# Attention transfers in program order, output weights gated and split in the stage before, and the attention output split where it is merged: one change to a two-layer trunk kernel on one core

## The chip, the cores and the metric

The kernel runs on one core of one Trainium2 chip. The metric is the device time of one launch in microseconds (us). Before the change the median of three runs is 2780.15 us, with 2775.05 as the lowest and 2784.62 as the highest.

The engines are named as the profile names them: PE is TensorE's matrix unit, PEld its weight loads, DVE is VectorE, ACT is ScalarE, POOL is GpSimd, SP is SyncE, which does little here but issue transfers. SPq and POOLq are the queues of transfers that SP and GpSimd issue.

## The reference: what must be computed

A sequence of 1024 tokens of width 1024 goes through two layers. Each layer has a token mixer and a dense MLP (1024 to 4096, squared ReLU, back to 1024). Every one of the four sub-layers is wrapped in the same way: `h = x * (1 + scale) + shift`, `x = LayerNorm(alpha * x + gate * f(h))`, where shift, scale and gate come from a conditioning vector. Layer 0 mixes with a gated MLP (mixer a), layer 1 with attention (mixer b). The change touches mixer b alone:

```
qkv = (h @ w_qkv)                      # 3 patterns x (q, k, v) x 16 heads x 64
for each pattern g (window, dilation) in (128,1), (512,4), (2048,16):
    s = q k^T / 8 + ALiBi bias          # 128 queries x 256 keys a block
    m = max(s);  p = exp(s - m);  l = sum(p)
    o_g = (p / l) v;   lse_g = m + log(l)
o = sum_g softmax_g(lse) * o_g          # the merge of the three patterns
y = o @ w_out;  x = LayerNorm(alpha * x + gate * y)
```

All is fp32. A matrix product is made of three passes in a rounded format: each operand is split into a high part (a cast on ACT) and a low part (a subtraction on DVE), and high*high, high*low and low*high are added up. The helper `split` (L100 to L104) issues the two instructions, L102 on ACT and L103 on DVE.

## The kernel before, in words

**The stages, in order of time.** Mixer a and its output projection; the MLP of layer 0 (`mlp(1)`); `values` (L1133), which makes v for all three patterns, and q and k of pattern 0, by a seven-product scheme; `attention` (L1279); the output projection of the attention; the MLP of layer 1 (`mlp(3)`). PE works in the order in which the program text issues. The order on the other engines is set by a scheduler, which takes an instruction when its operands are expected, unless the program pins it with `tc.keep_in_program_order`. The queue of an engine is then worked strictly in that order: an instruction that waits holds all that is behind it, transfers included.

**`values`.** The loop over `V_STEPS` (L1247) takes five blocks of seven products (numbered 1, 2, 5, 6, 7, 4, 3), each product four m-steps, each m-step twelve matmuls. After an m-step `evict` (L1217) either copies the sum to `vpart` (ACT, products 1, 5 and 6) or finishes it: an add on DVE, a split into a tile `vs` (two buffers, pool `parted`), and a store from GpSimd's queue to `v_dram` or `qk_dram` (L1233, L1240). The right-hand weights come through `raw_tile` buffers (two of tag "raw", three of tag "res").

**`attention`.** Eight pairs of heads times three patterns, in the order g = 0, 2, 1, make 24 groups of 8 slots, 4 slots for a head. Each slot has two half positions, and `at(slot, pos)` hangs a step on one. For head e of a group starting at slot `base`:
- `scores(m)` at base + 4e + m: four matmuls into `sc` (L1454, L1455), a bias add with row minimum on DVE into p (L1461), an exponential on ACT (L1463). For m = 0 it also issues the bias row on GpSimd (L1443), just ahead of its first use.
- `transposes(m)` (L1486) and its split into `pThi`, `pTlo` at base + 4e + w + 2, second half, where w is 0 to 3; `weighted(m)` (the `pv` matmuls, L1510, then the sum into `oT`, L1519 and L1520) two slots or more later. For g = 0 the last two m share one half slot (w = 3 for both).
- `statistics` (L1530) at base + 9 stores the row maxima and sums; for g = 0 they go through a transpose into `pstat` first (L1534 to L1536).

Between these steps a generator `project` is stepped: it loads the q and k weights of the coming groups (`unit`, L347), splits them and multiplies (`psq`, `psk`, L1366). A table `due` says how far it must be by a slot; its last entry is `last_group - 2`, with `last_group` = 184, the first slot of the last group.

**The merge** (`merge`, L1546) of a head pair begins when its three patterns are through. Steps on the slots of the next groups: `read` of the statistics, `late maths` for the three weights (L1567 to L1577), a store to `w_dram`, `spread`, which reads them back as rows `bc` across 64 partitions, and ten steps of scaling and adding on DVE (L1601, L1605). The sum of pairs 0 to 6 is stored to `o_dram` in fp32.

**The affine rows.** During the first groups GpSimd multiplies and adds the LayerNorm rows of the residual (L1637 load, two L1642 operations of 128x1024, L1643 store, eight rows one after the other).

**The output projection.** `OutRows` (L400) works on the eight 128-row units of `b_w_out`. `begin` does units 0 to 3 for tokens of the first half; its matmuls (`psd_wo`, L389) are stepped one at each half slot of the last group. `go_on` (L427) does the second half with units 0 and 1, then 2 and 3, then units 4 to 7 on both. A unit is loaded raw, multiplied by the row `gate_2` (GpSimd, L1688 for units 0 to 3, L356 for 4 to 7), and split (`wo_hi`, `wo_lo`). `prepare` (L1652) and `staged_rows` (L1701) load o from `o_dram` and split it into `oTs`. Units 6 and 7 have buffers `late_w`.

Of the kernel before, what the change touches and what calls it, by code (L numbers as in the profile page):

```python
# [10 lines left out]
F32 = mybir.dt.float32  # L11
# [6 lines left out]
P = 128  # L18
# [17 lines left out]
def trunk(ctx: ExitStack, tc: tile.TileContext, x, c, ada_w, ada_b, ln_g, ln_b, a_w_in, a_b_in,  # L36
# [168 lines left out]


# [140 lines left out]
    def unit(src, name, gate=None, pinned=False, lo_engine=V, to=None, raw=None):  # L347
        if raw is None:
            raw = wts.tile([P, D], F32, name=f"{name}_raw", tag="raw", bufs=2)[:]
        if src.shape[0] == P:  # L350
            nc.sync.dma_start(raw, src)
        else:
            nc.sync.dma_start(raw.rearrange("p (k n) -> p k n", n=P), src.rearrange("(k p) n -> p k n", p=P))
# [46 lines left out]
    class OutRows:  # L400
# [3 lines left out]
        def __init__(self, stat, weight, gate, res, prepare, name, raws={}):  # L404
            self.units = {}

            def load(ch):
                self.units[ch] = [unit(weight[k * P : (k + 1) * P, :], f"{name}_{k}", gate, ch > 1, raw=raws.get(f"w{k}"))
                                  for k in (2 * ch, 2 * ch + 1)]
# [10 lines left out]
            self.load, self.part, self.prepare, self.res, self.raws = load, part, prepare, res, raws  # L420
# [6 lines left out]
        def go_on(self):  # L427
# [6 lines left out]

            part((0,), 1)
            self.prepare(2)
# [4 lines left out]
            self.prepare(3)  # L441
            self.load(3)
            add(4, 5)
            part((2, 3), 0)
# [3 lines left out]
    def mixer_a():  # L448
        nonlocal ada_p, vec
        with ExitStack() as ph:  # L450
# [175 lines left out]
            with ExitStack() as a2:  # L626
# [9 lines left out]
                out = OutRows(uzT, a_w_out[0], gate, res, prepare, "wout")  # L636
# [435 lines left out]
    v_dram = [dram.tile([S, N_PAIRS, 4 * HEAD], F32, name=f"v_{g}") for g in range(3)]  # L1072
    qk_dram = [dram.tile([2 * N_PAIRS, 2, HEAD, S], F32, name=f"{n}_0") for n in "qk"]
# [59 lines left out]
    def values(before, right, ahead):  # L1133
# [3 lines left out]
        with ExitStack() as ph:  # L1137
# [104 lines left out]

            for n, (of, p) in enumerate(V_STEPS):
                while name[p] not in built:
                    next(stream)
                for m in range(4):
# [32 lines left out]
    def attention(form):  # L1279
        nonlocal vec  # L1280
        o_dram = dram.tile([N_PAIRS - 1, P, S], F32, name="o_dram")
# [3 lines left out]
        with ExitStack() as ph:  # L1285
# [55 lines left out]
            def project():  # L1341
# [3 lines left out]
                def load(n, X):  # L1345
                    hp, g = order[n]
                    c0 = g * 3 * D + X * D + hp * P
                    return unit(b_w_qkv[0, :, c0 : c0 + P], f"w{'qk'[X]}_{hp}_{g}", raw=raw_u[:])
# [34 lines left out]
            def load_qk(n):  # L1383
                hp = order[n][0]
                q, k = ([wts.tile([P, S], F32R, name=f"{nm}{e}_{hp}_0", tag=tag) for e in range(2)] for nm, tag in (("q", "whi"), ("k", "wlo")))
                for e in range(2):
                    rows = [d[2 * hp + e].rearrange("s c t -> (s c) t") for d in qk_dram]
                    nc.sync.dma_start(k[e][:].bitcast(F32), rows[1])
                    for i in range(2):
                        nc.sync.dma_start(q[e][64 * i : 64 * i + 64, :].bitcast(F32), rows[0][0:64])  # L1390
                    nc.sync.dma_start(zlo[e][0:64, :].bitcast(F32), rows[0][64:P])
# [14 lines left out]
            def attend(n, oT_of):  # L1406
# [6 lines left out]
                def load_v(e):  # L1413
# [4 lines left out]
                    if g == 0:  # L1418
                        nc.sync.dma_start(dst, src.rearrange("(t p) c -> p t c", p=P))
                    elif g == 1:  # L1420
                        for i in range(2):
                            nc.sync.dma_start(dst[:, i::2, :], src.rearrange("(i p r) c -> i p r c", i=2, r=4)[i])
                    else:
                        for b in range(2):
                            nc.sync.dma_start(dst[64 * b : 64 * b + 64], src.rearrange("(i b a) c -> b i a c", b=2, a=8)[b])
# [7 lines left out]
                for e in range(2):  # L1433
# [4 lines left out]
                    def scores(m, e=e, h=h, rows=rows, probs=probs, st=st):  # L1438
                        if m == 0:
                            if e == 0:  # L1440
                                my["stat"] = qp.tile([P, 2, 2, NT], F32, name=f"stat_{hp}_{g}", tag="stat", bufs=3)
                            st["bias"] = qp.tile([P, width], F32, name=f"bias_{h}_{g}", tag="bias")
                            G.tensor_scalar(st["bias"][:], far if g == 2 else near,  # L1443
                                            -8.0 * DILATION[g] * 2.0 ** (-8.0 * (h + 1) / N_HEADS), 1.0, ALU.mult, ALU.mult)
# [76 lines left out]

                    for m in range(4):
# [285 lines left out]
```

## Time and profile before

| | |
|---|---|
| median of three runs | 2780.15 us (2775.05 to 2784.62) |
| the profiled execution | 2781.12 us |
| its span in the trace | 2779.4 us |
| PE busy, in us and as a share of the span | 2668.7, 96% |
| DVE busy | 2036.6, 73% |
| ACT busy | 1419.5, 51% |
| POOL busy | 238.3, 9% |
| transfers | 483.78 MB, 174 GB/s mean |

The profile has one page for the whole span (busy time by engine, forty slices, the costliest groups of instructions by line) and views that can be asked of the trace: the waits of an engine by what ended them, busy times in chosen stretches with the granted clock of PE (1.00 is full speed), the chain of work that ended last, and a timeline of one engine. In the trace of before, `values` runs from about 995 to 1382 us, the slots of the attention from there to about 2060, the output projection to about 2145. A group of 8 slots takes some 26 us, so a slot takes about 3.25 us, and `last_group` begins at about 2026 us.

### The profile page before, as it was taken

The page shows a single profiled execution, that of the slowest core. Times are in us where ns is not written, and L with a number is a line of the kernel's source. Part 1 is how long each engine was busy: PE and PEld are TensorE (multiplying, and loading weights), DVE is VectorE, ACT ScalarE, POOL GpSimd, SP SyncE. Part 2 cuts the span into 40 slices and gives each one's busy share as a digit, 9 for nine tenths or more (in the row PEclk, how much of TensorE's full clock was granted, in tenths as well). Part 3 has the DMA queues.
Part 4 walks back from the last instruction along what each step waited for, and adds up shares of the span by engine and source line. Part 5 has one row for each costly group of instructions (what it writes and reads, how often), then busy time and mean ns, then how long its engine had stood idle before and what let it go on. Part 6 is the DMA issues. An engine that isn't in the chain of part 4 may idle for free.

```text
span 2779.4 us, 36657 instructions
## 1 busy us (share of the span) xinstructions
PE 2668.7 (96%) x12858; PEld 2222.1 (80%) x12858; DVE 2036.6 (73%) x3638; ACT 1419.5 (51%) x2655; POOL 238.3 (9%) x261
## 2 busy tenths in 40 slices
PE   6999999999999999999997999999988999999998
PEld 5787788887888878888886888878877788878887
DVE  6777698777877787655555777777768975668887
ACT  3354475555443464434364666666664755554332
POOL 1001000000000012211144011101120000000000
PEclk9999999999999999999998999999999999999999
DMA  7544347667846546655465455555444564486562
GB/s 258 162 124 124 114 138 235 214 219 263 315 139 195 169 144 205 207 201 201 154 202 147 124 135 123 138 131 131 120 127 159 166 209 153 159 284 212 172 200 90
DMA packets 344574, 483.78 MB, mean 174 GB/s; under 512 B 51981, under 2 KB 185525, under 8 KB 344389
## 3 DMA queue, kind: packets, MB, share of 16 engines
q1 hardware_dynamic: 329764, 430.05, 49.6%
q0 software_dynamic: 14624, 51.39, 5.4%
q8 instruction: 101, 1.65, 0.3%
q14 instruction: 85, 0.69, 0.1%
HBM read 355.44 MB, written 125.91 MB: 173 GB/s over the span
## 4 chain that ended last, share of the span: by engine, by line
PE 68%; DVE 14%; DMA 7%; ACT 5%; issue 3%; POOL 2%; SPq 0%; DVEq 0%; ACTq 0%; POOLq 0%
PE psd L955 21%; PE psv L1265 10%; PE psua L796 8%; PE psuc L796 4%; PE psu L368 3%; PE psq L1366 3%; PE psk L1366 3%; PE psd_wout L389 2%; PE psd_wo L389 2%; DMA adaw<-in_ada_w_dram 2%; PE psv L470 2%; PE psub L796 2%; PE pv L1510 2%; ACT p L1463 1%; POOL aff L1642 1%
## 5 line engine op out<-in xcount | busy, mean ns | idle before, releaser
L796 PE MATMUL psua<-right,left 128*128 128x512 f32 x1536 | 364.8, 391 | 0.3
L955 PE MATMUL psd<-rhi,lhi 128*128 128x512 f32 x896 | 349.2, 390 | 3.0 <-ACT part L827 3.0
L955 PE MATMUL psd<-rlo,lhi 128*128 128x512 f32 x896 | 348.9, 389 | 0.2
L955 PE MATMUL psd<-rhi,llo 128*128 128x512 f32 x896 | 348.6, 389 | 0.0
L796 PEld LDWEIGHTS psua<-right,left 128*128 128x128 f32 x1536 | 288.0, 188 | 62.5 <-DVE right L103 1.6
L1463 ACT ACTIVATE p<-p,stat 128x128 f32<-128x128 f32 (+1 forms) x384 | 170.7, 445 | 182.6 <-DVE stat L1461 168.5
L955 PEld LDWEIGHTS psd<-rhi,lhi 128*128 128x128 f32 x896 | 168.2, 188 | 38.8 <-ACT part L827 3.9
L955 PEld LDWEIGHTS psd<-rlo,lhi 128*128 128x128 f32 x896 | 168.2, 188 | 35.6 <-DVE rlo L103 1.1
L955 PEld LDWEIGHTS psd<-rhi,llo 128*128 128x128 f32 x896 | 168.2, 188 | 35.0
L796 PE MATMUL psuc<-right,left 128*128 128x512 f32 x768 | 187.5, 391 | 0.0
L128 DVE SCALAR_TENSOR_TENSOR adaacc<-adaw,silu_c,adaacc 128x512 f32<-128x512 f32 x168 | 132.2, 797 | 59.1 <-DMA adaw<-in_ada_w_dram 58.7
L796 PEld LDWEIGHTS psuc<-right,left 128*128 128x128 f32 x768 | 143.6, 188 | 30.0 <-DVE right L103 0.4
L103 DVE TENSOR_TENSOR left<-ws,left 128x512 fp32r<-128x512 f32 x128 | 87.8, 687 | 72.9 <-ACT left L102 71.3
L1461 DVE CUSTOM_DVE_ANT_0 p<-sc,bias 128x128 f32<-128x128 f32 (+1 forms) x384 | 119.0, 343 | 29.4 <-POOL bias L1443 20.2
L103 DVE TENSOR_TENSOR llo<-lraw,lhi 128x1024 fp32r<-128x1024 f32 x112 | 136.4, 1217 | 0.8 <-ACT lhi L102 0.8
L102 ACT CAST left<-ws 128x512 fp32r<-128x512 f32 x128 | 79.1, 620 | 96.5 <-DVE ws L717 86.6
L1366 PE MATMUL psk<-form_L,wk_hi 128*128 128x512 f32 x384 | 126.7, 411 | 0.0
L1366 PE MATMUL psq<-form_L,wq_hi 128*128 128x512 f32 x384 | 126.0, 410 | 0.0
L103 DVE TENSOR_TENSOR pTlo<-pT,pThi 128x384 fp32r<-128x384 f32 (+1 forms) x160 | 98.4, 620 | 32.1 <-ACT pThi L102 30.7
L102 ACT CAST rhi<-rraw 128x1024 fp32r<-128x1024 f32 x48 | 50.6, 1053 | 139.6 <-issue 114.1
L1520 DVE TENSOR_TENSOR oT<-oT,pv 64x512 f32<-64x512 f32 x96 | 65.8, 685 | 74.9 <-ACT oT L1519 74.1
L1265 PE MATMUL psv<-vrhi,form_S 128*128 128x512 f32 x384 | 119.2, 389 | 0.0
(311 smaller groups left out, 6478.1 us busy)
## 6 DMA issues: line engine op xcount, KB each, us to landing
lraw<-forms SPq DMA_DIRECT2D x112, 512.0 KB
adaw<-in_ada_w_dram SPq DMA_DIRECT2D x192, 256.0 KB
up<-in_mlp_w_up_dram SPq DMA_DIRECT2D x64, 512.0 KB
forms<-s SPq DMA_DIRECT2D x128, 256.0 KB
rraw<-in_mlp_w_down_dram SPq DMA_DIRECT2D x64, 512.0 KB
forms<-part SPq DMA_DIRECT2D x96, 256.0 KB
v<-vs POOLq DMA_DIRECT2D x48, 512.0 KB, 3.3
vraw<-in_b_w_qkv_dram SPq DMA_DIRECT2D x42, 512.0 KB
```

The costliest lines, as they stand in the source:

```text
L102: first = A.copy(hi, src) if hi_engine is A else hi_engine.tensor_copy(hi, src)
L103: return first, lo_engine.tensor_tensor(lo, src, hi, op=ALU.subtract)
L128: ins = V.scalar_tensor_tensor(acc[:], raw[:], silu_c[:, k : k + 1], acc[:], ALU.mult, ALU.add)
L368: T.matmul(dst, s[a], m[b], start=(n == 0), stop=(n == last))
L389: T.matmul(p[:], stat[a][:, k, o : o + P], u[b][:, w], start=n == 0, stop=n == count - 1)
L796: T.matmul(acc, w[:, a, k, :], right[p][:, b, k, :], start=p in (1, 2, 5) and k + a + b == 0, stop=k == 3 and a == 1, skip_group_check=True)
L955: ins = T.matmul(sums[kind, m][:], l[a][:, k, m * P : (m + 1) * P], r[b][:, k, :], start=p in (1, 5, 2, 3) and kp + k + a + b == 0, stop=k ...
L1265: T.matmul(acc, stat, mov, start=p in (1, 2, 5) and kp + k + a + b == 0, stop=kp == 1 and k == 1 and a == 1, skip_group_check=True)
L1366: T.matmul(p[:], wu[a][:, k * P : (k + 1) * P], h_op(k, half, b), start=k + c_ == 0, stop=k == KD - 1 and c_ == 2)
L1461: V.tensor_tensor_reduce(out=pr[:, 0:w], in0=scb[:, sl], in1=st["bias"][:, width - w :], scale=-0.125, scalar=3e38, op0=ALU.add, op1=ALU.m ...
L1463: A.activation(pr[:, 0:w], pr[:, 0:w], AF.Exp, bias=nm, scale=-1.0, accum_out=l)
L1520: V.tensor_tensor(dst, dst, pvs[b][main, :], op=ALU.add)
```

## The change

It has these parts.

1. **`in_turn`.** All transfers of the attention that SP issues (weights of q and k, q and k of pattern 0, v, the statistics, the merge's stores and reads, o) are pinned to program order on SP's queue.
2. **Output weights beside v.** In blocks 1 to 4 of `values`, a table `side` hangs steps on m-steps: load half of the gate row, load two 128-row units by 512 columns of `b_w_out` (512 KB, eight such loads), multiply them by the gate on GpSimd (two operations of 128x512 a load), split them into two tiles of tag "vs" (the tag that `evict` uses, two buffers as before), and store both from GpSimd's queue to a new tensor `wo_dram`. At the end of the attention `fetch` only loads a ready high and low part. The raw loads, the gate multiplications and the splits of the units at the end are gone.
3. **o split in the merge.** A new step `part` makes high and low halves of the merged o (two ACT casts, two DVE subtractions of 128x512 for each of seven pairs); `o_dram` holds both. The loads of o (`fetch_o`) go straight to `oTs`; `prepare` splits pair 7 alone.
4. **The order at the end.** `OutRows` takes `fetch` and a list `ends`: for the attention, `go_on` does units 4 and 5 on the first half, then splits pair 7, then units 6 and 7. `begin` is stepped at two of three half slots, and `project` may run until `last_group - 0.5`.
5. **The bias row** is a step of its own, two slots ahead of the scores that use it.
6. **Last transposes of pattern 0** (m = 3), and the weighted sum behind them, come half a slot later; the statistics half a slot to a slot later, and with them `read` (half a slot; for the last pair half a slot earlier) and `spread` (half a slot).

```diff
+    def in_turn(dst, src):
+        tc.keep_in_program_order(nc.sync.dma_start(dst, src))
...
@@ OutRows.go_on
+            early = len(self.ends) == 1
             part((0,), 1)
-            self.prepare(2)
+            if early:
+                self.prepare(2)
             self.load(2)
             add(0, 1)
             part((1,), 1)
             add(2, 3)
-            self.prepare(3)
+            if early:
+                self.prepare(3)
             self.load(3)
             add(4, 5)
-            part((2, 3), 0)
+            part(self.ends[0], 0)
+            if not early:
+                self.prepare(3)
+                part(self.ends[1], 0)
             add(6, 7)
@@ values
+            side = {}
+            for block in range(1, 5):
+                half, k0 = (block - 1) % 2, 4 * ((block - 1) // 2)
...
+                def load_pair(box, k, cols):
+                    box[k] = raw_tile(f"wo_raw_{k}")[:].rearrange("p (k n) -> p k n", n=HALF)
+                    nc.sync.dma_start(box[k], b_w_out[0, k * P : (k + 2) * P, cols].rearrange("(k p) n -> p k n", p=P))
+                def gate_pair(box, k):
+                    for i in range(2):
+                        G.tensor_tensor(box[k][:, i, :], box[k][:, i, :], box["gate"][:], op=ALU.mult)
+                def split_pair(box, k, cols):
+                    hi, lo = (parted.tile([P, 2, HALF], F32R, name=f"wo_{m}_{k}", tag="vs") for m in ("hi", "lo"))
+                    split(hi[:], lo[:], box.pop(k))
+                    for m, t in enumerate((hi, lo)):
+                        nc.gpsimd.dma_start(wo_dram[m, k : k + 2, :, cols].rearrange("k p n -> p k n"), t[:].bitcast(F32))
+                put(-1, 2, load_gate, box, half, cols)
+                for i, (at_load, at_gate, at_split) in enumerate((((-1, 2), (0, 0), (0, 2)), ((1, 2), (2, 0), (2, 2)))):
...
                     evict(of, p, m)
+                    for f in side.get((n, m), ()):
+                        f()
@@ attend
-                            st["bias"] = qp.tile([P, width], F32, name=f"bias_{h}_{g}", tag="bias")
-                            G.tensor_scalar(st["bias"][:], far if g == 2 else near, ...
+                    @at(max(base + 4 * e - 2, 0), 0)
+                    def bias(h=h, st=st):
...
-                        at(base + 4 * e + w + 2, 1)(lambda m=m, f=transposes: f(m))
-                        at(base + 4 * e + max(w, 1) + 4, 1)(lambda m=m, f=weighted: f(m))
-                @at(base + 9, 0)
+                        t2 = 2 * w + 5 + (g == 0 and m == 3)
+                        for f, n2 in ((transposes, t2), (weighted, max(t2, 7) + 4)):
+                            at(base + 4 * e + n2 // 2, n2 % 2)(lambda m=m, f=f: f(m))
+                @at(base + (10 if g == 0 else 9), int(g > 0 and n < len(order) - 1))
                 def statistics():
@@ merge
+                def part(_, half):
+                    w = slice(half * HALF, (half + 1) * HALF)
+                    for x_ in split(box[2][:, w].bitcast(F32R), box[1][:, w].bitcast(F32R), box[0][:, w]):
+                        in_order(x_)
+                    if half:
+                        for m, t in enumerate((box[2], box[1])):
+                            in_turn(o_dram[hp, m], t[:])
@@ the end of attention
-            staged_unit(0, (-10, 0), (-6, 1), (-5, 1))
...
-            staged_rows(1, 1, (-1, 0), 1)
+            def fetch(k):
+                parts = [wts.tile([P, D], F32R, name=f"wo_{k}_{m}", **(dict(tag="raw", bufs=2) if k == 3 else dict(tag=f"w{m}")))[:]
+                         for m in ("hi", "lo")]
+                for m, t in enumerate(parts):
+                    in_turn(t.bitcast(F32), wo_dram[m, k])
+                return parts
...
+            @at(last_group - 6, 1)
             def output():
+                ending["oT"] = [act_pair(f"oTs_{half}") for half in range(2)]
+                out = ending["out"] = OutRows(ending["oT"], fetch, Residual(2), prepare, "wo", ((2,), (3,)))
+                out.units[0] = [fetch(k) for k in range(2)]
+                out.units[1] = [fetch(k) for k in (2, 3)]
+            at(last_group - 3, 0)(lambda: fetch_o(0, 4, 0))
+            at(last_group, 1)(lambda: fetch_o(4, N_PAIRS - 1, 0))
+            at(last_group + 2, 0)(lambda: fetch_o(0, N_PAIRS - 1, 1))
-            due = ((0, 14), (16, 70), (24, 92), (last_group - 2, 512))
+            due = ((0, 14), (16, 70), (24, 92), (last_group - 0.5, 512))
@@ the loop over slots
-                        next(ending["begin"], None)
+                            begin()
+                        if (2 * n + pos) % 3:
+                            next(ending["begin"], None)
```

The matmuls are the same in number and shape.

More of the change, by code (lines that the diff above doesn't have):

```diff
@@ L400, in trunk, with __init__ @@
     class OutRows:
-        def __init__(self, stat, weight, gate, res, prepare, name, raws={}):
+        def __init__(self, stat, fetch, res, prepare, name, ends):
             self.units = {}
             def load(ch):
-                self.units[ch] = [unit(weight[k * P : (k + 1) * P, :], f"{name}_{k}", gate, ch > 1, raw=raws.get(f"w{k}"))
-                                  for k in (2 * ch, 2 * ch + 1)]
+                self.units[ch] = [fetch(k) for k in (2 * ch, 2 * ch + 1)]
             def part(chs, half):
@@ L1665, in pinned_split @@
-            def pinned_split(hi, lo, src):
-                for x_ in split(hi, lo, src):
-                    tc.keep_in_program_order(x_)
-            @at(last_group - 8, 1)
-            def gate_row():
-                ending["oT"] = []
-                ending["gate"] = vec.tile([P, D], F32, name="gate_2", tag="oT", bufs=4)
-                nc.sync.dma_start(ending["gate"][:], gate_dram[2].partition_broadcast(P))
-                ending["out"] = OutRows(ending["oT"], b_w_out[0], ending["gate"], Residual(2), prepare, "wo", ending)
-                ending["out"].units.update({0: [], 1: []})
@@ L1718, in attention, with prepare @@
[L1718 to L1723 removed]
+            def prepare(_):
+                for half in range(2):
+                    o_hi, o_lo = ending["oT"][half]
+                    split(o_hi[:, N_PAIRS - 1, :], o_lo[:, N_PAIRS - 1, :], oTs["sum"][:, half * HALF : (half + 1) * HALF])
+            def fetch(k):
[4 more added lines that the diff above has]
+                return parts
@@ L1777, in trunk @@
         done.open(ph, 1)
-        late = pool(ph, "late", 1)
-        for n in ("w6", "w7", "o6"):
-            out.raws[n] = late.tile([P, D], F32, name=f"late_{n}")[:]
         out.go_on()
```

128 lines of the change are left out of this document (45 added, 83 removed).

## The prediction, on record before the changed kernel ran

> **What bounds the kernel now.** I read the page's head first, then busy times in stretches, then what PE waited for from 1382 to 2190 us, where nearly all of the change lies.
>
> ```profile
> PE 2668.7 (96%) x12858; PEld 2222.1 (80%) x12858; DVE 2036.6 (73%) x3638; ACT 1419.5 (51%) x2655; POOL 238.3 (9%) x261
> ```
>
> PE is busy for 96% of the span, and the change takes no matmul away. So there are two things to win: time in which PE stands, and time in which it runs at a lower granted clock. The stretches show where both are (columns: the stretch and its length, then busy us and instructions of PE, PEld, DVE, ACT, POOL, then the granted clock, the DMA share, GB/s).
>
> ```profile
> 1100.00:1382.00 282.00, 281.79 (x1243) 233.46 (x1244) 168.01 (x196) 115.42 (x162) 45.86 (x82) 1.00 0.57 188
> 1470.00:1500.00 30.00, 16.11 (x86) 13.55 (x86) 7.73 (x28) 8.27 (x27) 14.98 (x13) 0.80 0.33 107
> 1500.00:2000.00 500.00, 479.66 (x2886) 417.55 (x2886) 370.19 (x1086) 332.93 (x942) 58.16 (x69) 0.98 0.51 131
> 2000.00:2050.00 50.00, 43.30 (x230) 36.22 (x229) 45.10 (x97) 33.83 (x91) 19.01 (x10) 0.90 0.52 162
> 2050.00:2100.00 50.00, 39.56 (x185) 32.49 (x185) 30.41 (x58) 20.04 (x42) 5.26 (x2) 0.90 0.44 117
> 2100.00:2150.00 50.00, 49.22 (x232) 40.26 (x231) 43.00 (x103) 24.57 (x36) 0.00 (x0) 1.00 0.44 149
> ```
>
> In `values` (first row) PE has no idle time at all: whatever is added there can only cost. The attention has a hole at 1470 to 1500 (PE idle 30 − 16.1 = 13.9 us), small losses along 1500 to 2000 (20.3 us), and a bad end at 2000 to 2100 (6.7 + 10.4 = 17.1 us). PE's waits name the causes (total us, times, longest):
>
> ```profile
> PE sc L1454 <- DVE stat L1461: 13.9, 2, 12.1
> PE pT L1486 <- DVE pTlo L103: 13.1, 10, 2.4
> PE pv L1510 <- DVE pTlo L103: 7.2, 13, 1.3
> PE psd_wo L389 <- DVE acc L395: 7.1, 2, 6.3
> PE pstat L1534 <- DVE pTlo L103: 2.3, 4, 1.0
> PE sc L1454 <- DMA q<-q: 1.9, 1, 1.9
> ```
>
> The clock is the second loss. These are the stretches in which it was granted at half:
>
> ```profile
> 1474.40:1477.80 3.40, 3.40 (x13) 2.92 (x13) 1.88 (x7) 2.43 (x8) 0.59 (x1) 0.50 0.47 154
> 1491.50:1505.20 13.70, 5.79 (x20) 5.12 (x21) 5.26 (x13) 5.38 (x14) 8.68 (x8) 0.50 0.24 89
> 1829.40:1836.20 6.80, 6.03 (x21) 5.29 (x22) 3.59 (x11) 3.36 (x11) 0.00 (x0) 0.50 0.54 110
> 2023.90:2034.10 10.20, 9.45 (x31) 7.57 (x31) 10.12 (x19) 7.77 (x18) 4.67 (x4) 0.50 0.67 216
> 2068.30:2071.70 3.40, 3.28 (x9) 2.79 (x10) 3.34 (x5) 1.07 (x2) 3.40 (x2) 0.50 0.07 27
> 2092.20:2099.00 6.80, 3.42 (x8) 2.75 (x9) 6.12 (x9) 1.22 (x2) 0.00 (x0) 0.50 0.70 229
> ```
>
> Work done at half clock would have taken half the time, so I price the clock at half of PE's busy time there: 1.7, 2.9, 3.0, 4.7, 1.6 and 1.7 us. That is an estimate; weight loads and short matmuls may not scale. Each stretch follows a wait, and the first follows one of only 13.9 − 12.1 = 1.8 us.
>
> [...]
>
> **The change part by part**, against the profiled execution's 2781.12 us, which is 0.97 above the median of the runs.
>
> *Start.* The first scores waited 1.9 us for q. In the changed order some 23 more projection matmuls stand ahead of them, about 5 us at 282 / 1243 = 0.23 each: gone. −2 (0 to −2).
>
> *Bias rows.* The hole at 1488 is GpSimd's:
>
> ```profile
> DVE p L1461 <- POOL bias L1443: 20.2, 2, 15.9
> 1398.52 1.40 POOL L1376 TENSOR_SCALAR q<-q 64x1024 fp32r<-64x1024 f32 x1 [7.13 <-ACT q L102]
> 1402.64 0.54 POOL L1637 DMA_DIRECT2D aff<-spill  x1
> 1483.45 0.59 POOL L1643 DMA_DIRECT2D spill<-aff  x1 [0.41 <-POOL aff L1642]
> 1488.99 0.54 POOL L1637 DMA_DIRECT2D aff<-spill  x1 [4.94 <-DMA spill<-aff]
> 1498.27 0.42 POOL L1443 TENSOR_SCALAR bias<-dist 128x256 f32<-128x256 f32 x1
> 1507.32 2.40 POOL L1642 TENSOR_TENSOR aff<-aff,aff_b 128x1024 f32<-128x1024 f32 x1
> ```
>
> DVE wanted the row at about 1498.7 − 15.9 = 1482.8, but it stood behind a whole affine row (load, two operations, store). In the changed order it stands ahead of that row's load, right behind the store of 1483.45, and the affine chain's first load stands ahead of the q copies, which waited until 1398.5: it goes out right behind the last v store and the first bias rows, near 1392 instead of 1402.6, and the chain begins some 10 us earlier. The row would then be there by about 1475. What goes: 13.9 idle plus 1.7 + 2.9 of clock, 18.5 at most. The next bias row of this kind is now between the two operations of the last affine row (the one that ended at 1509.7), wanted some four slots of 3.25 later, 1496: if the chain is 10 us earlier it comes at 1497. That leaves a small wait. −17 (0 to −19).
>
> *Pattern 0's last transposes and the statistics.* They wait 13.1 + 2.3 us on DVE's split two steps before, plus 3.0 of clock at 1829. Half a slot is 1.6 us, and most of these waits are at most 2.4. But DVE is busy 370 and ACT 333 of 500 us there, and each of seven merges gets two casts and two subtractions more, 9 us of ACT and 10 of DVE over 630 by the same shape's rows in `values`: part of the wait returns as pv behind the same split. −8 (−2 to −16).
>
> ```profile
> L103 DVE TENSOR_TENSOR vs<-vpart,vs 128x512 fp32r<-128x512 f32 x48 | 33.0, 688 | 29.1 <-ACT vs L102 29.1
> L102 ACT CAST vs<-vpart 128x512 fp32r<-128x512 f32 x48 | 29.8, 621 | 85.3 <-DVE vpart L1225 43.4 <-DMA v<-vs 18.9 <-DMA k<-vs 13.1
> ```
>
> *The end.* The chain of work there, and what the removed operations cost:
>
> ```profile
> 2060.26 3.99 DMA st_dram<-stat
> 2064.73 4.32 DMA late_w<-in_b_w_out_dram
> 2079.31 4.48 DMA bc<-w_dram
> 2085.12 0.98 DVE wo_lo L103
> 2089.44 1.14 DVE wo_lo L103
> 2095.58 27.76 PE psd_wo L389 x114
> L103 DVE TENSOR_TENSOR wo_lo<-wo_raw,wo_hi 128x1024 fp32r<-128x1024 f32 x6 | 7.5, 1254 | 1.3 <-ACT wo_hi L102 1.3
> L102 ACT CAST wo_hi<-wo_raw 128x1024 fp32r<-128x1024 f32 x6 | 6.2, 1040 | 0.1
> L1688 POOL TENSOR_TENSOR wo_raw<-wo_raw,gate 128x1024 f32<-128x1024 f32 x4 | 10.3, 2582 | 10.4 <-DMA wo_raw<-in_b_w_out_dram 8.7 <-DMA gate<-gate_dram 1.7
> L103 DVE TENSOR_TENSOR oTs<-oraw,oTs 128x512 fp32r<-128x512 f32 x12 | 13.2, 1112 | 3.2 <-ACT oTs L102 3.2
> ```
>
> The last statistics (2060) go through two round trips to memory and the scaling, and PE had too little else to do until the weight halves came in between (2085, 2089): it stood 6.3 us. The change takes from this stretch eight wo splits (8 × 1.25 = 10 us DVE, 8.3 ACT) and twelve oTs splits (13.2 DVE), and lets 22 us of matmuls (96 at 0.23) on units 0 and 1 run ahead of the first one that needs unit 4. The loss is 17.1 idle plus 4.7 + 1.6 + 1.7 of clock = 25; of this what the softmax chain itself sets remains. Against it stand transfers: four weight units in two parts (4 MB), o in two parts (7 MB), v and o stores (2.5), 13.5 MB between slots 178 and 187. At 271 GB/s (quoted next) that is 50 us from 2009 on, and the last v is wanted about 51 us in, since all stand in program order on SP's queue. Also a wait that is now pinned on SP (a statistics read on its store) holds all loads behind it.
>
> ```profile
> 2016.00:2028.00 12.00, 7.64 (x42) 6.62 (x42) 10.41 (x26) 9.12 (x23) 4.64 (x2) 0.83 0.80 271
> ```
>
> −10 (+8 to −18): about half of what the waits allow, since stepping `begin` at two of three half slots leaves three slots near 184 with less matmul work.
>
> *Beside v.* New: eight pairs, each two gate operations on GpSimd (half of 2.58 each), a cast (1.04), a subtraction (1.25) and two stores of 512 KB. All hide under PE's 282 us if they come in time: DVE goes from 168 to some 178, ACT from 115 to 124, transfers from 188 to some 230 GB/s (12.6 MB more). Their cover is PE's psum banks and the two `vs` tiles, each of which stands still until its store has landed (the stores of `vs`):
>
> ```profile
> DMA to landing us min/median/max: 2.8/3.7/8.9
> ```
>
> A pair is through in 1.0 + 1.2 + 0.5 + 3.7 = 6.4 us; the next eviction wants a tile two m-steps later, 2 × 12 × 0.23 = 5.4. One buffer is free before that, so a wait of some tenths, covered by a bank. +3 (0 to +10).
>
> [...] Row: oTs took DVE 1112 ns beside busy GpSimd, where plain 128x512 ones take 0.69. By it 16 × 1.29 = 21 us of GpSimd would cost DVE up to 0.6 × 21 = 13; as DVE has 114 free, `values` would move to the upper end, +10, and the sum to 2754.
>
> *After the attention.* `mlp(3)`'s loads come earlier or as before; its stages are bound by PE. 0.
>
> Sum: −2 − 17 − 8 − 10 + 3 = −34, **2747 us**. Likeliest case's own range 2732 to 2760.
>
> **The rivals.**
>
> *Slower: ScalarE stands behind the weight cast in `values`.* Load to cast is four m-steps, 10.9 us; the load (4.32 at 2064.73) and two gate operations (2.58) need 6.9. So it decides from 4 us of delay on. If the 512 KB buffer comes free four m-steps late, because wo_raw now takes a place in the same ring as v's weights, the gate, the cast and all copies of psums behind it on ACT, and GpSimd's v stores, are 6.9 late; eight times 6.9 = 55: 2747 − 3 + 55 = 2799. For it: PE has no slack there. Against: GpSimd is busy 46 of 282 and five raw buffers go round.
>
> *The bias wait moves only.* If the affine chain doesn't start earlier, the row inside the last affine row is about 10 us late: the term is −5, sum 2759.
>
> *Transfers jam at the end.* At 200 GB/s 13.5 MB take 67 us against 51: 16 us late, partly under matmuls; the term becomes 0 to +8, sum 2757 to 2765.
>
> *The moved waits come back,* because DVE and ACT, not the slots, set the pace, at 1500 to 2100: only start and bias remain, with values: −16, 2765. With a poor bias term as well it does nothing: 2777.
>
> **How the numbers follow.** Likeliest case 0.50; better than it (all terms near their best, 2720 to 2732) 0.08; bias moves 0.12; jam 0.12; waits come back 0.10, a third of that near 2777; slower 0.08. A measurement can tell about 0.3%, 8.3 us, from no change: faster means below 2772. Faster 0.50 + 0.08 + 0.12 + 0.12 + 0.06 = 0.88, from which I take 0.05 for several small losses together; same 0.07; slower 0.10. The range 2726 to 2780 leaves out the slower case and half of the better one.
>
> **What would show it.** Right: no PE idle of over 4 us at 1470 to 1500, no DVE wait on a bias row above 3; pT waits down from 13.1 to under 6; 2000 to 2100 with PE busy over 88 of 100; `values` as long as before to 3 us. Wrong: PE in `values` waiting for ACT or a DMA; PE waiting for v or wo loads in the last group; bias waits that moved; half clock elsewhere.

## The result, and the profile after

The changed kernel takes 2825.62 us (median of four runs, 2820.51 to 2828.04) against 2782.29 for the kernel before in the same comparison: a ratio of 1.0158, with a 95% interval of 1.0132 to 1.0184. The forecast was 2747 us, so the sign was wrong, and the time lies outside the range. The profiled execution took 2828.04 us, 46.9 more than that of before.

First: in which stage? Three rows a kernel from the view of one tile's instructions give the start of the first and of the last matmul of a stage (last two numbers before the semicolon): the last one of `values`, the last scores, the last of the output projection (`psv`, `sc` and `psd_wo`).

Before:

```profile
L1265 PE MATMUL psv<-vrhi,form_S x384: 389/389/389, 1176.5 to 1383.0; 128*128 128x512 f32 x192
L1455 PE MATMUL sc<-k,qlo x256: 272/274/415, 1422.2 to 2058.6; 128*128 128x128 f32 x128
L389 PE MATMUL psd_wo<-wo_hi,oTs x256: 387/389/797, 2027.4 to 2149.6; 128*128 128x512 f32 x128
```

After:

```profile
L1311 PE MATMUL psv<-vrhi,form_S x384: 387/389/500, 1183.9 to 1393.6; 128*128 128x512 f32 x192
L1500 PE MATMUL sc<-k,qlo x256: 272/276/415, 1436.7 to 2111.3; 128*128 128x128 f32 x128
L394 PE MATMUL psd_wo<-wo_hi,oTs x256: 387/389/794, 2092.0 to 2195.8; 128*128 128x512 f32 x128
```

To the end of `values` the changed kernel loses 10.6 us (1393.6 − 1383.0). From there to the last scores it takes 717.7 instead of 675.6, 42.1 more. The end of the projection takes 84.5 instead of 91.0, 6.5 less. What is left over, 630.5 against 629.8 us of span, is the same. So the loss is in the attention, where the forecast had no term against it at all. The same stretch in one row each, before and after (columns as in the prediction):

```profile
1383.00:2058.60 675.60, 632.32 (x3729) 547.87 (x3727) 474.95 (x1351) 429.77 (x1202) 130.23 (x122) 0.97 0.52 141
1393.60:2111.30 717.70, 645.53 (x3699) 553.87 (x3698) 469.49 (x1351) 430.69 (x1201) 103.35 (x116) 0.95 0.54 145
```

PE stands 72.2 us instead of 43.3, so 28.9 of the 42.1 us are idle time. The other 13.2 are longer busy time, which fits the lower granted clock: by the prediction's estimate (half of the busy time at half clock) the clock cost 30 us here against 14 before.

Shorter stretches of after, for those of before:

```profile
1470.00:1500.00 30.00, 26.82 (x146) 22.80 (x145) 15.96 (x51) 17.41 (x51) 11.06 (x9) 0.90 0.75 211
1500.00:1560.00 60.00, 44.49 (x249) 38.41 (x248) 35.20 (x100) 29.03 (x81) 20.64 (x19) 0.85 0.47 116
1500.00:1900.00 400.00, 353.67 (x2058) 304.47 (x2057) 272.57 (x786) 243.20 (x680) 46.14 (x58) 0.95 0.50 124
2112.00:2196.00 84.00, 82.23 (x391) 67.53 (x390) 65.33 (x149) 34.17 (x58) 0.00 (x0) 1.00 0.56 189
```

Before, the stretch from 1500 to 1900 reads

```profile
1500.00:1900.00 400.00, 383.58 (x2302) 334.21 (x2301) 294.87 (x862) 266.40 (x755) 48.89 (x56) 0.98 0.51 130
```

The hole at 1470 to 1500 is smaller (3.2 idle, before 13.9), but there is a new one at 1500 to 1560 (15.5). In 400 us PE does 2058 matmuls instead of 2302, with DVE and ACT less busy too. No engine has become the bound: all wait more. PE's waits from 1382 to 2190:

```profile
PE pstat L1586 <- DVE pTlo L103: 21.9, 8, 3.2
PE pT L1531 <- DVE pTlo L103: 19.9, 9, 11.8
PE pv L1555 <- DVE pTlo L103: 11.0, 17, 1.2
PE pv L1555 <- ACT pThi L102: 7.7, 9, 2.9
PE sc L1499 <- DVE stat L1506: 4.0, 4, 2.0
...
PE psq L1414 <- ACT wq_hi L102: 2.4, 1, 2.4
```

The waits of the projection on `acc` are gone (7.1 before). The waits on the scores have shrunk from 13.9 to 4.0. But `pstat` went from 2.3 to 21.9, and an 11.8 us wait of pT is new. The long one is a bias row's (under "Bias rows" below). What feeds the others is seen one engine further back, in ACT's own waits from 1382 to 2130 us. Before:

```profile
ACT wq_hi L102 <- DMA w_raw<-in_b_w_qkv_dram: 2.4, 2, 2.2
```

After:

```profile
ACT wk_hi L102 <- DMA w_raw<-in_b_w_qkv_dram: 19.5, 11, 6.8
ACT wq_hi L102 <- DMA w_raw<-in_b_w_qkv_dram: 17.7, 8, 3.8
```

The casts of the q and k weights wait 37 us for their loads. They stand in ACT's queue ahead of exponentials and of `pThi`, and DVE's `wq_lo` stands in DVE's queue ahead of `pTlo`: DVE's own waits for these casts (`wq_hi`, `wk_hi`) went from 18.1 to 52.7 us. One such load, followed on three engines of the changed kernel. DVE frees the only raw buffer:

```profile
1651.95 1.23 DVE L103 TENSOR_TENSOR wk_lo<-w_raw,wk_hi 128x1024 fp32r<-128x1024 f32 x1 [1.26 <-ACT wk_hi L102]
```

SP issues the next weights far behind that:

```profile
1655.09 1.22 SPq L208 DMA_DIRECT2D v<-v  x2
1658.06 1.94 SPq L208 DMA_DIRECT2D st_dram<-stat  x2
1666.38 1.26 SPq L208 DMA_DIRECT2D o_dram<-bc  x2
1667.68 0.44 SPq L208 DMA_DIRECT2D k<-k  x1
...
1673.71 1.58 SPq L208 DMA_DIRECT2D v<-v  x2
1675.90 0.73 SPq L208 DMA_DIRECT2D w_raw<-in_b_w_qkv_dram  x1
```

And ACT has them at:

```profile
1686.56 1.05 ACT L102 CAST wq_hi<-w_raw 128x1024 fp32r<-128x1024 f32 x1 [2.47 <-DMA w_raw<-in_b_w_qkv_dram]
```

The buffer is free at 1653.2; the load goes out 22.7 us later, behind the store of o, whose operands come late (SP waits 6.3 us for them), and a burst of q, k and v, and needs 10.7 us to arrive. Before, the same step took 0.03 us:

```profile
1663.45 1.22 DVE L103 TENSOR_TENSOR wq_lo<-w_raw,wq_hi 128x1024 fp32r<-128x1024 f32 x1 [0.35 <-ACT wq_hi L102]
```

```profile
1664.70 0.37 SPq L353 DMA_DIRECT2D w_raw<-in_b_w_qkv_dram  x1
```

### The profile page after: what moved, and what is told of

Its sections match the earlier page's. It is cut to its first block, busy times and chain, and to the rows that moved or that the text cites. A ratio compares the mean times of both kernels' runs of the same rounds, so it can differ in the third digit from the quotient of the medians.

```text
span 2826.3 us, 36722 instructions
## 1 busy us (share of the span) xinstructions
PE 2689.5 (95%) x12858; PEld 2230.8 (79%) x12858; DVE 2039.2 (72%) x3646; ACT 1418.4 (50%) x2655; POOL 240.6 (9%) x285
## 3 DMA queue, kind: packets, MB, share of 16 engines
q8 instruction: 101, 1.65, 0.3%
## 5 line engine op out<-in xcount | busy, mean ns | idle before, releaser
L1414 PE MATMUL psk<-form_L,wk_hi 128*128 128x512 f32 x384 | 134.7, 433 | 0.0
L102 ACT CAST lhi<-lraw 128x1024 fp32r<-128x1024 f32 x112 | 117.3, 1048 | 5.9 <-PE psua L806 3.7
```

The lines of the kernel that those rows point to most:

```text
L102: first = A.copy(hi, src) if hi_engine is A else hi_engine.tensor_copy(hi, src)
L1414: T.matmul(p[:], wu[a][:, k * P : (k + 1) * P], h_op(k, half, b), start=k + c_ == 0, stop=k == KD - 1 and c_ == 2)
```

## The experiments

Theory P: the pinning to program order brings the q and k weights late. Theory S: the statistics of pattern 0, moved to base + 10, find both psum buffers taken by the last two transposes. Theory L: the added splits of o load DVE and ACT. Times are medians, and so are differences in us; ratios, with 95% intervals, are to the kernel before, run in the same comparison (2782.3 to 2782.7 us), and can differ a little from the quotient of the medians.

**1. The statistics back at base + 9, in the changed kernel**

```diff
-                @at(base + (10 if g == 0 else 9), int(g > 0 and n < len(order) - 1))
+                @at(base + 9, int(g > 0 and n < len(order) - 1))
```

> The changed kernel with one step moved back: the statistics of pattern 0 are again at base + 9, first half, ahead of the transposes that share its psum buffers, instead of base + 10 behind two of them. Theory S (the statistics transpose is the third user of two psum buffers within one slot and waits 2.6 us at each pair, after which the clock is at half for 3.4 us or more): the pstat waits (21.9 us) go to under 4, each pair is about 4 us shorter, and the time falls from 2825 by 25 to 30, to 2795-2800. Theory P (the pinned transfers bring the q and k weights late) and theory L (the added splits of o load DVE and ACT) both expect at most 6 us less, since the next wait behind the same split takes its place.

Measured: 2813.73 us, ratio 1.0101 (1.0072 to 1.0131): 12 us less than the changed kernel, not 25 to 30. The pstat waits fell to 1.9, as S says, but the time came back only in part: waits of sc rose from 4.0 to 9.8 and those of pT from 19.9 to 23.8, since the weights were still late. S is one part, not the cause.

**2. The transfers unpinned, in the changed kernel**

```diff
-        tc.keep_in_program_order(nc.sync.dma_start(dst, src))
+        nc.sync.dma_start(dst, src)
```

> The changed kernel with the transfers of the attention left to the scheduler on SP's queue, as before; all else as changed. Theory P: ACT's waits for w_raw in the attention (37 us over 19 casts) go to under 8, the groups of pattern 0 (30.1 us each, before 26.6) fall to about 27, and the time falls by 20 to 25, to 2800-2805; the pstat waits stay. Theory S: at most 6 us less, as the pstat waits stay at 22. Theory L: no change beyond 3 us.

Measured: 2772.26 us, ratio 0.9961 (0.9946 to 0.9975): 53 us less, twice what P itself had expected, and faster than before. ACT's waits of 37 us became

```profile
ACT wq_hi L102 <- DMA w_raw<-in_b_w_qkv_dram: 2.7, 3, 1.1
ACT wk_hi L102 <- DMA w_raw<-in_b_w_qkv_dram: 2.2, 2, 1.2
```

and the pstat waits stayed at 17.6, so this gain is not S's. P underrated the price; part of it is clock, an estimated 12 us (below). Theory L is not borne out either: with the added splits of o still in, the stretch from the last matmul of `values` to the last scores takes 666.1 us, less than the 675.6 before. What the splits cost by themselves no run shows.

**3. The output weights beside v, in the kernel before**

The table `side` of the change is put into `values` of before, with the store to `wo_dram`, which nothing reads; the kernel's end is unchanged.

```diff
+            side = {}
...
                     evict(of, p, m)
+                    for f in side.get((n, m), ()):
+                        f()
```

> The kernel before with the output weights also gated, split and stored beside v, as in the change; nothing reads them, and the end of the attention is as before, so this work is extra. If values lost its 11 us to that part alone (GpSimd stands 7 us at a gate multiplication whose gate row comes late, k stores stand behind it, ACT waits 8.9 us for their buffer), the time is 2781 + 11 = 2792, with a PE wait of over 3 us in values. If the loss came from the rest of the change (other transfers, projection matmuls moved to its end), it is 2781 to 2784.

Measured: 2794.19 us, ratio 1.0034 (1.0018 to 1.005): 11.5 us more by the medians, 5 to 14 by the interval. In the profiled execution, the slowest of ten, `values` ends 9.5 us later than before (1392.5 against 1383.0), close to the 10.6 of the changed kernel, with one PE wait of 3.3 us for `vpart`. So the loss of `values` belongs to this part. The same execution lost another 10 us in the attention, where PE's waits of sc on DVE were 20.9 instead of 13.9; whether that belongs to the part too stays open.

**4. The bias row two slots ahead, in the kernel before**

```diff
-                            st["bias"] = qp.tile([P, width], F32, name=f"bias_{h}_{g}", tag="bias")
-                            G.tensor_scalar(st["bias"][:], ...
+                    @at(max(base + 4 * e - 2, 0), 0)
+                    def bias(h=h, st=st):
```

> The kernel before with one part of the change: the bias row is a step of its own, two slots ahead. The prediction's term: the hole of 12 us at 1487 goes, 2781 - 17 = 2764. Rival: the wait only moves, since GpSimd's queue is in order and the affine rows take the same time; PE then stands about 10 us some 15 to 40 us later, and the time is 2776 to 2781.

Measured: 2769.56 us, ratio 0.9937 (0.9916 to 0.9957): 13 us less by the medians, 12 to 23 by the interval, between the two. The waits of sc on DVE (13.9) are gone, but part of the hole moved to the next bias row: DVE still waits 7.4 us for bias rows, and pT's longest wait is 6.3 us instead of 2.4.

**5. Unpinned, and the statistics at base + 9**

Both edits of 1 and 2.

> The changed kernel with both taken back: transfers left to the scheduler, and the statistics of pattern 0 at base + 9. With the transfers unpinned the profile still has pstat waits of 17.6 us and some 20 us of half clock behind them. Theory S as a cost of its own: they go, the groups of pattern 2 fall from 30 to 27 us, and the time falls by 15 to 25 from 2772, to 2750-2757. If these waits only stand in for others on the same split (as they did with pinned transfers, where 20 us of waits returned 12), it falls by 5 to 12, to 2760-2767.

Measured: 2765.16 us, ratio 0.9932 (0.9914 to 0.9951): 7 us below run 2, in the smaller range. With the weights in time the pstat waits mostly stood in for others on the same split. This is the fastest version here and beats both kernels; its distance to run 4 is no larger than the spread of either.

**6. The gate row of `values` in its own buffer, on top of 5**

```diff
-            xp = pool(ph, "x_v", 9)
+            xp = pool(ph, "x_v", 8)
...
-                    box["gate"] = x_tile(f"gate_2_{half}")
+                    box["gate"] = hold.tile([P, HALF], F32, name=f"gate_2_{half}", tag="gate")
...
-                put(-1, 2, load_gate, box, half, cols)
+                put(-4, 0, load_gate, box, half, cols)
```

> The same as the unpinned kernel with the statistics at base + 9, and beside v the gate row has a buffer of its own, loaded one product sooner (and one x buffer fewer). If values lost its 11 us because GpSimd stood at a gate multiplication whose row came late, the wait of over 4 us near 1141 goes and values is 7 to 9 us shorter than in the run beside it. If the two vs tiles shared with the weights are the cause, values is shorter by at most 3.

Measured: 2769.36 us, ratio 0.9942 (0.9926 to 0.9958). The wait of 4.0 us in `values` of run 5 is gone; in its place stand four waits on the same `vpart`, and one on `form_S`, which run 5 didn't have:

```profile
PE psv L1311 <- DVE vpart L1236: 4.1, 4, 2.0
PE psv L1311 <- ACT form_S L102: 2.1, 1, 2.1
```

The wait went with the row's lateness, as said, but taking it away gained no time: `values` wasn't 7 to 9 us shorter. One x buffer fewer may have cost it; the two can't be told apart from this run.

**7. The transfers pinned, in the kernel before**

```diff
-                    nc.sync.dma_start(k[e][:].bitcast(F32), rows[1])
+                    in_turn(k[e][:].bitcast(F32), rows[1])
...
```

and so for all thirteen places of `attention`, and for the loads of w_raw.

> The kernel before with the transfers of the attention pinned in program order on SP's queue and nothing else. Theory P: the pinning costs as much by itself as it did in the changed kernel, where taking it away gained 53 us: 2782 + 30 to 55 = 2812-2837, with ACT waits for w_raw of over 25 us. If it only costs in company of the other parts (moved statistics, split of o), the time is within 10 us of 2782.

Measured: 2819.57 us, ratio 1.0122 (1.01 to 1.0143): 37 us more from order alone, without any other part of the change. ACT's waits for w_raw are 14.3 + 7.8 = 22.1 us, a little under what P named, and PE's waits of sc on DVE rise from 13.9 to 31.0:

```profile
PE sc L1458 <- DVE stat L1465: 31.0, 14, 10.7
```

**8. The loads of the q and k weights alone unpinned, in the changed kernel**

```diff
-                    return unit(b_w_qkv[0, :, c0 : c0 + P], f"w{'qk'[X]}_{hp}_{g}", raw=raw_u[:], pinned_load=True)
+                    return unit(b_w_qkv[0, :, c0 : c0 + P], f"w{'qk'[X]}_{hp}_{g}", raw=raw_u[:])
```

> The changed kernel with the loads of the q and k weights alone left to the scheduler; all other transfers of the attention stay pinned. Theory P in its narrow form (a weight load stands on SP's queue behind a statistics read or a weights store that waits, and ACT's cast waits for it): nearly all comes back, 2772 to 2785, w_raw waits under 8 us. If the harm is done by the v, q and k loads of pattern 0 or by the merge's own round trips, the time stays above 2805.

Measured: 2781.64 us, ratio 0.9994 (0.998 to 1.0008): 44 of the 53 us come back through these loads alone, though v, q, k, the statistics and the merge stay pinned. The waits:

```profile
ACT wq_hi L102 <- DMA w_raw<-in_b_w_qkv_dram: 1.0, 2, 0.8
ACT wk_hi L102 <- DMA w_raw<-in_b_w_qkv_dram: 0.8, 1, 0.8
```

This is P in its narrow form.

**9. The last affine row later, on top of 5**

```diff
-                at(2 + 3 * i, 0)(lambda i=i: affine_load(i))
-                at(3 + 3 * i, 1)(lambda i=i: affine_row(i))
+                at(2 + 3 * i + 3 * (i == 7), int(i == 7))(lambda i=i: affine_load(i))
+                at(3 + 3 * i + 3 * (i == 7), 1)(lambda i=i: affine_row(i))
```

> The unpinned kernel with the statistics at base + 9, and the last affine row (load and multiplication) three and a half and three slots later, so that the bias row which stood between that row's load and its first operation on GpSimd's queue stands ahead of the load. If the 8.1 us that PE still stands near 1500 are that bias row's wait, they fall to under 2 and the time by 8 to 11 from the 2765 of the run without it, to 2754-2757. If DVE is late there for another reason, or if the later row holds up the first merge instead, the time stays within 3 us of 2765.

Measured: 2766.43 us, ratio 0.9948 (0.9932 to 0.9965): no gain over run 5. PE's wait went from 8.1 to 4.8 and DVE's longest wait for the row from 4.7 to 1.5, but a pstat wait of 3.2 came in its place, and DVE was late for another reason, shown in the last section.

**10. The merge's transfers alone unpinned, in the changed kernel**

```diff
-                        in_turn(w_dram[hp, g].rearrange("e (q n) -> q e n", n=NT), a[:, g].rearrange("p (e n) -> p e n", n=NT))
+                        nc.sync.dma_start(w_dram[hp, g].rearrange("e (q n) -> q e n", n=NT), a[:, g].rearrange("p (e n) -> p e n", n=NT))
```

and so for the merge's other transfers.

> The changed kernel with the merge's transfers alone left to the scheduler (reads of the statistics, stores and reads of its weights, stores of o); q and k weights, v, q, k and the statistics' stores stay pinned. If the weights stand behind the merge's waits (SP waited 103 us for the merge's maths before its stores), most of the 44 us that freeing the weights gave comes back: 2780 to 2795. If they stand behind the waits of the v and q loads for their buffers and of the statistics for their scores just as much, half or less comes back: 2805 or more.

Measured: 2823.95 us, ratio 1.015 (1.013 to 1.0171): nothing came back. By the expectation that would speak for the v and q loads and the statistics, but the run doesn't separate what it was meant to: in its trace the queue's order hardly changed. The store of o (1749.03) and the merge's weights (1699.45, 1701.44) still go out ahead of the next `w_raw` (1757.99 and 1708.54); only reads of the statistics moved. So freeing these transfers didn't free the loads behind them, and which of the transfers ahead holds a load longest stays open.

**11. Only the last transposes of pattern 0 half a slot later, in the kernel before**

```diff
-                        at(base + 4 * e + w + 2, 1)(lambda m=m, f=transposes: f(m))
-                        at(base + 4 * e + max(w, 1) + 4, 1)(lambda m=m, f=weighted: f(m))
+                        t2 = 2 * w + 5 + (g == 0 and m == 3)
+                        for f, n2 in ((transposes, t2), (weighted, max(t2, 7) + 4)):
+                            at(base + 4 * e + n2 // 2, n2 % 2)(lambda m=m, f=f: f(m))
```

> The kernel before with the last transposes and weighted sum of pattern 0 half a slot later, the statistics left where they were. The prediction's term: pT waits fall from 13 to under 6 us, 2782 - 8 = 2774. Rival: the wait on the same split comes back at pv or one step later, 2780 to 2784.

Measured: 2785.39 us, ratio 1.0014 (0.9997 to 1.0031): no gain. The waits changed names:

```profile
PE pT L1486 <- DVE pTlo L103: 11.0, 10, 2.7
PE pv L1510 <- ACT pThi L102: 8.6, 7, 2.8
...
PE pstat L1535 <- DVE pTlo L103: 5.1, 4, 2.3
```

**12. The same, with the statistics of pattern 0 at base + 10**

```diff
-                @at(base + 9, 0)
+                @at(base + (10 if g == 0 else 9), 0)
```

> The same with the statistics of pattern 0 at base + 10 as in the change. Theory S: their transpose then finds both psum buffers taken, seven waits of 2 to 3 us and half clock behind them: 10 to 20 us above the run with the statistics left in place. If this harm came only in company of late weights, it is within 5 us of it.

Measured: 2785.04 us, ratio 1.0013 (0.9998 to 1.0027). The pstat waits come to 19.6, nearly as in the changed kernel, and cost nothing over run 11: pT (7.4 instead of 11.0) and pv (7.2 instead of 12.5) wait less, and the rest doesn't show in the time. So S costs nothing in the kernel before; in company of the rest of the change the step was worth 12 and 7 us (runs 1 and 5).

## Why the prediction was wrong, point by point

**The step that failed: the pinned order got no term.** The forecast treated part 1 as a matter of the end ("a wait that is now pinned on SP (a statistics read on its store) holds all loads behind it") and priced no queue in the groups before that. The order of the change was to be compared with that of before on SP as it was on GpSimd: for each load, when its buffer comes free, and what waits ahead of it. The loads that mattered were those of the q and k weights, with their single raw buffer. Pinning costs 37 us on the kernel before (run 7), and unpinning gives 53 back on the changed one (run 2), 44 of it through the weights (run 8). Without it the forecast's sign was right: 2772.26, and 2765.16 with the statistics back. Its size wasn't: −10 in run 2 instead of −34. The terms as measured below, 0 − 13 + 0 − 6.5 + 10.6, add up to about −9, though not all of them come from the same run.

**Start, −2.** The wait of sc on q went from 1.9 to 0.3, but psq now waits 2.4 for its weights. Nothing was gained.

**Bias rows, −17.** By itself the part gave 13 (run 4), inside its range. In the changed kernel the outcome of the second rival came true as well: the wait moved. Rows of GpSimd's timeline:

```profile
1399.56 0.53 POOL L1695 DMA_DIRECT2D aff<-spill  x1
1414.48 2.41 POOL L1700 TENSOR_TENSOR aff<-aff,aff_g 128x1024 f32<-128x1024 f32 x1 [14.39 <-DMA aff<-spill]
1528.10 0.39 POOL L1570 TENSOR_SCALAR bias<-dist 128x256 f32<-128x256 f32 x1
```

The first affine load did go out ahead of the q copies, but it came 14.4 us later, so the chain's first operation started 4.5 us later than before (1409.9), not 10 earlier. `values` had ended 10.6 later; counted from its end, the chain starts 6 us earlier. It then took longer: 114 us from the start of its first operation to that of its last, before 97. The row between the last two operations came at 1528.5; DVE waited 8.8 us for it, and PE 11.8.

**Pattern 0's last transposes and the statistics, −8.** Nothing was gained (runs 11 and 12: +2.8 and +2.4, neither clear of zero). "Part of the wait returns" was right in kind; all of it did. PE's order is fixed there, and a step moved by half a slot waits for the same split under another name.

**The end, −10.** The mechanism was right, and its size nearly: 6.5 less in the changed kernel. PE's idle time in the last 84 us is 1.8 and the clock 1.00 throughout. In the 100 us that answer to 2000 to 2100 (58.6 us ahead of the last scores and 41.4 behind them: 2052.7 to 2152.7) PE is busy for 94.2 us, before 82.9; the forecast asked for over 88. No transfer jam came: PE's longest wait for v was 1.65 us, at 2031.

**Beside v, +3.** The mechanism of the first rival, at a fifth of its price: a late load, then GpSimd, then ACT, then PE. The rows, on GpSimd:

```profile
1135.01 3.51 POOL L1274 TENSOR_TENSOR wo_raw<-wo_raw,gate 128x512 f32<-128x512 f32 x2 [6.98 <-DMA gate<-gate_dram]
1138.47 2.46 POOL L1251 DMA_DIRECT2D k<-vs  x4
```

on ACT:

```profile
1143.62 0.62 ACT L102 CAST vs<-vpart 128x512 fp32r<-128x512 f32 x1 [8.86 <-DMA k<-vs]
```

and on PE:

```profile
1145.62 0.75 PE L1311 MATMUL psv<-form_L,vrhi 128*128 128x512 f32 x1 [4.39 <-DVE vpart L1236]
```

The forecast watched the weights' load; the gate row behind it was later, and the stores of k stood behind the multiplication. This wait and the 3.4 us at half clock behind it are about 6 of the 10.6 us; PE's other waits for DVE's `vpart` come to 2.6. The part alone (run 3) costs about the upper bound of its range, 10.

**The clock.** In the changed kernel the waits of pstat that ended at 1721.6 (2.54 us) and at 1808.0 (2.58) were each followed by a stretch at half clock. The 3.4 us ahead of each stretch, then the stretch:

```profile
1719.10:1722.50 3.40, 0.90 (x6) 0.81 (x7) 2.20 (x8) 2.67 (x7) 0.00 (x0) 1.00 0.01 3
1722.50:1725.90 3.40, 3.40 (x13) 2.91 (x12) 2.32 (x9) 1.46 (x5) 0.00 (x0) 0.51 0.02 5
1804.50:1807.90 3.40, 0.72 (x5) 0.58 (x5) 1.99 (x8) 2.16 (x8) 1.04 (x1) 1.00 0.17 49
1807.90:1811.30 3.40, 3.32 (x10) 2.74 (x11) 3.40 (x10) 1.51 (x5) 0.00 (x0) 0.50 0.03 7
```

By the prediction's estimate (half of the busy time) these cost 1.7 us each. From 1000 to 2150 us the trace of before holds 7 stretches at half clock and that of after 15, of 3.4 to 13.7 us each; within one trace their starts lie whole multiples of 3.413 us apart. Cut at these starts and every 3.413 us from them, the two traces hold, at full clock, 17 windows in which PE was busy for 45% or less: all were followed by half clock. Of the 20 windows at 46% to 68%, 5 were, and of the 597 above none. The prediction's wait of 1.8 us lay within one such window (1471.0 to 1474.4, PE busy 1.58 of 3.40). (The prediction's list of such stretches before lacks one, 3.4 us at 1515.3.)

From the last matmul of `values` to the last scores the changed kernel's trace has 75 us at half clock, against 38 before; PE was busy for 60 us of the 75. In run 2 the mean granted clock over the whole span is 0.987, against 0.983 in the changed kernel. At half clock that is some 72 of 2776.3 us, against some 96 of 2826.3; half of the difference, an estimate that takes PE as busy throughout, is 12 us of the 53 that run 2 gained.

## What to carry to other kernels

Before pinning transfers to program order, take each load with a single buffer, note when that buffer comes free, and read what stands ahead of it on its queue: a load that was issued at once (0.03 us) went out 22.7 us late here, and the order alone cost 37 us. Where PE waits several times for the same split, moving one waiting step may only rename the wait, as it did here; look one and two engines back for what made the split late. And a gain that comes from clearing a queue has to be checked for the next item of that queue: the bias row's wait moved once, and once more.

## What the runs showed of the hardware that was not expected

In four places a tiny operation on DVE took 1.28 to 2.35 us and ended with an operation of GpSimd's, where in the traces of before and after others of the same lines took at most 0.18. In run 9, GpSimd's two affine operations:

```profile
1501.15 2.39 POOL L1700 TENSOR_TENSOR aff<-aff,aff_g 128x1024 f32<-128x1024 f32 x1 [6.12 <-DMA aff<-spill]
1503.62 2.37 POOL L1700 TENSOR_TENSOR aff<-aff,aff_b 128x1024 f32<-128x1024 f32 x1
```

and DVE beside them:

```profile
1501.34 2.24 DVE L1619 TENSOR_TENSOR mm<-mst 128x16 f32<-128x16 f32 x1
1503.61 0.69 DVE L103 TENSOR_TENSOR pTlo<-pT,pThi 128x512 fp32r<-128x512 f32 x1
1504.22 1.80 DVE L1620 TENSOR_TENSOR mm<-mm,mst 128x16 f32<-128x16 f32 x1
```

The operations on 128x16 take 2.24 and 1.80 us and end with GpSimd's (1503.58 against 1503.54, 1506.02 against 1505.99); the split between them, which reads one operand from psum, takes its usual 0.69. With GpSimd quiet, the same line took 0.18 us (at 1518.80 in the changed kernel's trace):

```profile
1518.80 0.18 DVE L1619 TENSOR_TENSOR mm<-mst 128x16 f32<-128x16 f32 x1
```

Two more operations of these two statements ran beside GpSimd's in the kernel before: they took 1.28 and 2.35 us and ended at 2070.39 and 2073.27, GpSimd's at 2070.36 and 2073.24. In the traces of before and after none without GpSimd beside it took over 0.18.

The prediction priced GpSimd's work beside DVE as a slowdown by 0.6 of the overlap, from a mean of 1112 ns over twelve splits `oTs`. That mean mixes two cases: nine took 0.67 to 0.69 us, and three, which began during an operation of GpSimd's, 1.77 to 2.86 and ended about 0.5 us after it. (Two of the nine, at 2034.03 and 2070.32, began so as well; there GpSimd's operations lasted 3.21 and 2.93 us instead of 2.4.) The four small operations ended within 0.04 us of GpSimd's. What sets the slowed operations apart from the others no run shows.
